# Expert outputs stored by slot, and finished tokens gathered, normed and written inside a hand-ordered expert stretch

## The chip, the cores and the metric

The kernel runs on one NeuronCore of one Trainium2 chip. What is judged is the device time of one execution in microseconds (us), the median of the runs. The engines are PE (TensorE, the matmuls), DVE (VectorE), ACT (ScalarE), POOL (GpSimd) and SP, which here only issues transfers. Each engine takes its own instructions in their written order: an instruction that waits holds up every one behind it on that engine, and nothing else until somebody waits for those.

## The reference

One decoder layer of 1024 tokens of 1024 numbers. Three sub-layers, each `x <- LayerNorm(alpha * x + f(x))`: a mixer (mLSTM and a pooling group), a cross-attention to 256 memory tokens, and a mixture of experts. The change touches the last one and its norm:

```
x = layer_norm(DEEPNORM_ALPHA * x + xa, ln_x_g, ln_x_b)
e = top-2 experts of each token (of 16), gate = their weights
hb = silu(xb @ w_gate[e]) * (xb @ w_up[e])      # 1024 -> 256, per block of 128 tokens of an expert
y  = hb @ w_down[e]                             # 256 -> 1024
ff = sum over the token's two experts of gate * y
x  = layer_norm(DEEPNORM_ALPHA * x + ff, ln_moe_g, ln_moe_b)
```

The norm takes mean and variance over the 1024 numbers of a token, then scales by `g` and adds `b`.

## The kernel before, in words

The stages follow one another: input projection, mixer, memory keys and values, attention scores, attention output with routing, experts, third norm. `yd` is an array in memory that the second norm fills with `alpha * x`.

Experts. Each expert takes its tokens in blocks of 128 slots. There are 24 fixed blocks: the eight busiest experts have two, the other eight one; experts are ordered by how many tokens they have, and a loop behind them (`For_i`, L1511) does what is left if an expert has more; here it makes no turn. Blocks 0 and 1 are done in the stage before; the loop over blocks 2 to 23 is the stretch that this text speaks of. One block is, in the order of its data:

- POOL gathers 128 rows of `xd` by the slot list (`xbs`, L994), PE transposes them (`tp_xb`), ACT rounds them into a high part (L1103) and DVE takes the rest as a low part (`xbT`, L1105);
- PE does 24 matmuls into `gup` (three for each product, high and low parts, L78 to L80), ACT the Silu (`hb`, L1118; called the gate below), DVE the product (L1119, "mult"), PE two transposes (`hp`, L1124, "flip"), ACT and DVE the two parts of the result (`hbT`, L74 and L75), and PE 12 matmuls into `yp`;
- ACT scales `yp` by the slots' weights (`y`, L1145), and POOL adds the rows to `yd` by token, in memory (L1146). Each of these additions waits until the one before has landed, as both write `yd`.

Beside that the weights come in: SP fetches 1 MB at a time into a ring of five buffers (`raw`, L834), and each buffer is split in two pieces into high parts (ACT, L74) and low parts (DVE, L75); a piece is 128x1024, an expert has six, and the loop's experts 84. In this loop the framework's scheduler sets the order of the instructions on each engine.

After the last block some twenty small steps on PE and DVE make the list of the blocks beyond the fixed ones (L1452 to L1485), each engine reads their number, and then the third norm runs: eight loads of `yd` into buffers (`yl`, L1573), statistics on DVE (L1541 to L1543) or ACT (L1545), the power -1/2 on POOL (L1554), the two passes over the row on DVE (L1556, L1558), ACT and POOL (L1564, L1566), and eight stores (L1568), in an order that a string lists by hand.

Of the kernel before, what the change touches and what calls it, by code (L numbers as in the profile page):

```python
# [43 lines left out]
def trunk_kernel(ctx: ExitStack, tc: tile.TileContext, a, out):
# [1401 lines left out]
    def extra_blocks():  # L1446
        def c16(name, n=NE, dtype=F32):
            return const.tile([NE, n], dtype, name=name)

# [29 lines left out]
        for k in range(8):  # L1479
            pe.matmul(lps[:1, :NE], pcol[:, :1], ohx[:, k, :], start=k == 0, stop=k == 7)  # L1480
# [9 lines left out]
    for n in range(2, len(blocks)):  # L1490
# [4 lines left out]
        if n + 1 < len(blocks):  # L1495
            parts = block_parts(gathered[n + 1], f"{n + 1}")
# [130 lines left out]
```

## Time and profile before

| | us |
|---|---|
| median of 3 runs | 996.57 |
| the runs | 992.66, 996.57, 996.59 |
| span of the profiled execution | 991.4 |
| of it the expert loop, up to the last matmul of block 23's first product and block 22's second | up to 939.7 |
| of it from the last small matmul on | 944.5 to 991.4 |
| PE, DVE, ACT, POOL busy in the span | 910.8, 584.9, 410.9, 304.2 |

The profile is of one execution. The page gives its span, from the first instruction to the last, and not the device time of that same execution; the median of the runs lies 5.2 us above the span, the lowest run 1.3. Times inside the span are counted from its start.

### The profile page before, as it was taken

How to read it: one execution, taken by the hardware profiler on the slowest of the kernel's cores; microseconds unless marked ns; L12 is line 12 of the kernel's file. 1: busy time of each engine (PE TensorE's matmuls, PEld its weight loads, DVE VectorE, ACT ScalarE, POOL GpSimd, SP SyncE). 2: the span in 40 equal slices, each digit the busy share in tenths (PEclk: the TensorE clock that was granted, in tenths of full speed). 3: DMA queues.
4: the chain of work that ended last, by engine and by line, in shares of the span. 5: the costliest groups of instructions: out<-in, count | busy, mean ns of one | idle time of the engine just before them, and what ended most of it. 6: DMA issues, size and time to landing. Idle time of an engine off the chain costs nothing. (4 is left out here: it accounts for less than half of the span.)

```text
span 991.4 us, 13027 instructions
## 1 busy us (share of the span) xinstructions
PE 910.8 (92%) x4841; PEld 774.9 (78%) x4841; DVE 584.9 (59%) x1154; ACT 410.9 (41%) x640; POOL 304.2 (31%) x221
## 2 busy tenths in 40 slices
PE   8999999999899999999999999987589999999910
PEld 8999778788677889998888888876468888888710
DVE  5300374546876785272224558979957677676528
ACT  5311432245422144352224432234237667767524
POOL 0211243226453314201111042325732323333226
PEclk9999999999999999999999999999799999999965
DMA  8200011113421357420001012173549898898364
GB/s 304 83 22 22 22 65 43 64 32 128 170 75 54 107 194 273 150 86 0 1 1 43 1 43 86 64 310 108 190 128 347 298 317 290 281 296 270 51 196 167
DMA packets 35439, 133.41 MB, mean 135 GB/s; under 512 B 6640, under 2 KB 8240, under 8 KB 29232
## 3 DMA queue, kind: packets, MB, share of 16 engines
q1 hardware_dynamic: 28464, 115.79, 32.3%
q0 software_dynamic: 6912, 16.79, 7.2%
q8 instruction: 38, 0.62, 0.2%
q14 instruction: 25, 0.20, 0.1%
HBM read 115.75 MB, written 25.20 MB: 142 GB/s over the span
## 5 line engine op out<-in xcount | busy, mean ns | idle before, releaser
L75 DVE TENSOR_TENSOR ew<-raw,ew 128x1024 fp32r<-128x1024 f32 x84 | 101.5, 1223 | 21.7 <-ACT ew L74 20.8
L74 ACT ACTIVATE ew<-raw 128x1024 fp32r<-128x1024 f32 x96 | 100.3, 1057 | 19.4 <-PE xa L80 9.7
L78 PE MATMUL gup<-ew,xbT 128*128 128x512 f32 x192 | 79.2, 412 | 0.0
L1146 POOL DMA_INDIRECT yd<-y,idx x22 | 41.5, 1884 | 122.2 <-ACT ew L74 46.2
L79 PE MATMUL gup<-ew,xbT 128*128 128x512 f32 x192 | 76.7, 399 | 0.0
L80 PE MATMUL gup<-ew,xbT 128*128 128x512 f32 x192 | 76.7, 399 | 0.0
L78 PE MATMUL zB<-xs,wb 128*128 128x512 f32 x192 | 76.5, 399 | 0.0
L80 PE MATMUL zB<-xs,wb 128*128 128x512 f32 x192 | 76.1, 396 | 0.0
L79 PE MATMUL zB<-xs,wb 128*128 128x512 f32 x192 | 75.0, 391 | 0.0
L78 PE MATMUL xa<-vws,T_p 128*128 128x512 f32 x128 | 53.9, 421 | 0.0
L78 PE MATMUL mixp<-wm,mx 128*128 128x512 f32 x128 | 53.2, 415 | 0.0
L79 PE MATMUL mixp<-wm,mx 128*128 128x512 f32 x128 | 50.9, 398 | 0.7 <-DVE wm L75 0.7
L79 PE MATMUL xa<-vws,T_p 128*128 128x512 f32 x128 | 51.4, 401 | 0.0
L80 PE MATMUL xa<-vws,T_p 128*128 128x512 f32 x128 | 51.3, 401 | 0.0
L80 PE MATMUL mixp<-wm,mx 128*128 128x512 f32 x128 | 50.9, 398 | 0.0
L78 PE MATMUL sc<-As,T_x 128*128 128x512 f32 x128 | 50.9, 398 | 0.0
L80 PE MATMUL sc<-As,T_x 128*128 128x512 f32 x128 | 50.4, 394 | 0.0
L79 PE MATMUL sc<-As,T_x 128*128 128x512 f32 x128 | 50.2, 392 | 0.0
L791 POOL TENSOR_TENSOR pss<-pss,nm 128x1024 f32<-128x1024 f32 x8 | 15.1, 1894 | 113.2 <-DVE nm L789 113.2
L80 PEld LDWEIGHTS gup<-ew,xbT 128*128 128x128 f32 x192 | 36.8, 192 | 8.5
L78 PEld LDWEIGHTS gup<-ew,xbT 128*128 128x128 f32 x192 | 37.0, 193 | 7.9 <-issue 0.6
L79 PEld LDWEIGHTS zB<-xs,wb 128*128 128x128 f32 x192 | 36.1, 188 | 8.9 <-issue 0.5
(447 smaller groups left out, 2505.2 us busy)
## 6 DMA issues: line engine op xcount, KB each, us to landing
raw<-in_wgu SPq DMA_DIRECT2D x32, 1024.0 KB, 8.2
raw<-in_wdn SPq DMA_DIRECT2D x16, 1024.0 KB, 7.4
raw_wk<-in_wkv SPq DMA_DIRECT2D x16, 512.0 KB, 4.5
wbr<-in_wB SPq DMA_DIRECT2D x12, 512.0 KB, 3.2
xt<-in_x SPq DMA_DIRECT2D x8, 512.0 KB, 3.2
raw_wq<-in_wxqT SPq DMA_DIRECT2D x8, 512.0 KB, 4.2
xd<-x2s SPq DMA_DIRECT2D x8, 512.0 KB, 3.3
yd<-xal SPq DMA_DIRECT2D x8, 512.0 KB, 2.8
```

Of the source, the lines that this page charges most:

```text
L74: act.activation(hi, src, AF.Copy)
L75: sub.tensor_tensor(lo, src, hi.bitcast(F32), op=ALU.subtract)
L78: pe.matmul(ps, lhi, rhi, start=first, stop=False)
L79: pe.matmul(ps, lhi, rlo, start=False, stop=False)
L80: pe.matmul(ps, llo, rhi, start=False, stop=last)
L791: pool.tensor_tensor(pr4, pr4, nm[:, 1, :, None].to_broadcast([P, H, M]), op=ALU.mult)
L1146: pool.indirect_dma_start(out=yd[:, :], out_offset=bass.IndirectOffsetOnAxis(ap=ix, axis=0), in_=y[:, :D], in_offset=None, bounds_check=T ...
```

## The change

Three things change, all of them from block 2 on; the stages ahead of it keep their work.

- Each block's `y` goes out with a plain store by SP, row by slot, to a new array `yb` of 24 * 128 rows (L1155). Nothing is added to `yd` in the fixed blocks any more.
- From block 4 on a list of some 95 small steps (`late_steps`) is dealt out over the agenda, 0.9 units apart. They work out for each token the two slots where its results lie and the rank of its later expert, sort the tokens by that rank, and write lists (`done`) of nine tiles of tokens: token numbers, first slots, second slots. Two of these steps put groups of small matmuls on PE (`invert`, 8; `listed`, 32), one makes a 128x1024 mask on DVE. The steps on the blocks beyond the fixed ones move here from the end.
- As soon as a tile's tokens have both results, POOL gathers their rows of `yd` and adds those of `yb` (L1458), DVE and POOL norm them (`stats` L593 to L595, the power L599, `vec1` L602, `vec2` L605), and POOL scatters them to the output (L1471). Tiles 8, 7, 6, 5 ("slow") add both `yb` rows in memory transfers and are normed in blocks 18, 19, 21 and 22; tiles 4, 3, 2, 1 ("fast") use freed weight buffers, fetch the second row apart and add it on DVE (`sum`, L1770), in blocks 22 and 23 and after. Tile 0, the tokens of the last expert, takes the last block's result from PSUM (`meet`, L1810).

The stretch is now ordered by an agenda: every step has a time in units (a block is 10 units long, block n starts at `10 * (n - 2)`), and on each engine the instructions stand in the order of these times.

The core of the diff:

```diff
@@ the store of a block @@
-        pool.indirect_dma_start(out=yd[:, :], out_offset=bass.IndirectOffsetOnAxis(ap=ix, axis=0), in_=y[:, :D], in_offset=None,
-                                bounds_check=T - 1, oob_is_err=False, compute_op=ALU.add)
+    def b_store(yp, gc, n):
+        sp.dma_start(yb[n * P:(n + 1) * P, :], b_scaled(yp, gc, f"{n}"))
@@ the gathers of a tile, and its store @@
+    def z_rows(y, src, ix, rows, add=False):
+        pool.indirect_dma_start(out=y, out_offset=None, in_=src[:rows, :], in_offset=bass.IndirectOffsetOnAxis(ap=ix, axis=0),
+                                bounds_check=rows - 1, oob_is_err=False, **(dict(compute_op=ALU.add) if add else {}))
+    def z_add(i, k, n):
+        z_rows(S["z", i], yb, done[:, 1 + k, i:i + 1], n * P, True)
+    def z_store(i):
+        pool.indirect_dma_start(out=out[:, :], out_offset=bass.IndirectOffsetOnAxis(ap=done[:, 0, i:i + 1], axis=0), in_=S["z", i],
+                                in_offset=None, bounds_check=T - 1, oob_is_err=False)
@@ two of the late steps @@
+        def invert():
+            for t in range(NT):
+                pe.matmul(li[:, :3 * NL], slot[:, t * P:(t + 1) * P], val[:, t, :, :].rearrange("p v k -> p (v k)"), start=t == 0, stop=t == NT - 1)
+        yield lambda: vec.tensor_tensor(slot[:, :1024].rearrange("p (t s) -> p t s", s=P), iota[:, None, :].to_broadcast([P, NT, P]),
+                                        rm[:, :, None].to_broadcast([P, NT, P]), op=ALU.is_equal)
@@ a block of the agenda @@
+    SPAN = 10.0
+    for n in range(2, NB):
+        B = start(n)
+        T0 = B - 4.2 if n > 2 else B - 4.0
+        at(T0, e_turn, n)
+        at(T0 + 1.0, e_hi, n)
+        at(T0 + 2.2, e_lo, n)
+        for j, o in enumerate((0.0, 0.7, 1.6, 2.3, 6.7, 7.4, 8.1, 8.8)):
+            at(B + o, e_hidden, n, j)
+        N = B + SPAN
+        at(N + 0.05, e_gate, n)
+        at(N + 0.5, e_mult, n)
+        at(N + 1.5, e_flip, n)
+        at(N + 1.7, e_fold, n)
+        if n < NB - 1:
+            at(N + 3.0, e_out, n, 0)
+            at(N + 4.4, e_out, n, 1)
+            at(N + 5.85, e_store, n)
+    places = [(start(n) + o) for n in range(3, NB) for o in (0.6, 2.0, 3.05, 4.1, 8.05)]
+    for n, step in enumerate(late_steps()):
+        at(start(4) + 5.0 + 0.9 * n, step)
@@ the tiles @@
+        at(B - 3.0 + shift if fast else B, z_x)
+        if fast:
+            at(B + 1.0 + shift, z_add, i, 0, n + 1)
+            at(B + 1.1 + shift, lambda: z_rows(S["zb", i], yb, done[:, 2, i:i + 1], (n + 1) * P))
+            at_z = B + 7.0 + shift
+            at(at_z, z_sum)
+        else:
+            at(B + 6.0, z_add, i, 0, n + 1)
+            at(B + SPAN + 6.0, z_add, i, 1, n + 1)
+            at_z = B + 2 * SPAN + 5.0
+    def z_vec(i, when):
+        at(when, lambda: S.update({("ln", i): ln_stats(S["z", i], f"n3_{i}")}))
+        at(when + 1.6, lambda: ln_pow(S["ln", i][1]))
+        at(when + 1.7, lambda: ln_vec1(S["z", i], S["ln", i][0], gb3))
+        at(when + 3.0, lambda: ln_vec2(S["z", i], S["ln", i][1], gb3))
+        at(when + 4.3, z_store, i)
+    for i, m in ((8, 8), (7, 9), (6, 10), (5, 11)):
+        z_vec(i, z_tile(i, last_of[m]))
+    for i, m, r in ((4, 12, 4), (3, 12, 3), (2, 13, 2), (1, 14, 1)):
+        z_vec(i, z_tile(i, last_of[m], True, fetch_order[r], 4.5 if i == 3 else 0.0))
@@ the last block @@
+        vec.scalar_tensor_tensor(y[:, o:o + 512], S["yp", NB - 1][:, o:o + 512], gc, y[:, o:o + 512], op0=ALU.mult, op1=ALU.add)
+        vec.bn_stats(S["st", 0][:, o // 512, :], y[:, o:o + 512])
```

Where the instructions stand, at three places.

DVE in block 22, before: from the mult of block 21 to that of block 22. `ew15` are the last expert's weights, `xbT` the low part of block 23's tokens, `hbT21` the low part of block 21's hidden row.

```order
L1119 TENSOR_TENSOR hb21_7825<-hb21_7825,gup21_7800 128x256
L75 TENSOR_TENSOR ew15_1_7915<-raw0_5517,ew15_1_7915 128x2x512
L75 TENSOR_TENSOR ew15_2_7918<-raw1_5519,ew15_2_7918 128x2x512
L75 TENSOR_TENSOR ew15_3_7945<-raw1_5519,ew15_3_7945 128x2x512
L1105 TENSOR_TENSOR xbT0_5705<-tp_xb23_7873,xbT0_5705 128x1024
L75 TENSOR_TENSOR hbT21_7859<-hp21_7856,hbT21_7859 128x256
L75 TENSOR_TENSOR ew15_4_7948<-raw2_5521,ew15_4_7948 128x1024
L75 TENSOR_TENSOR ew15_5_7951<-raw2_5521,ew15_5_7951 128x1024
L1119 TENSOR_TENSOR hb22_7909<-hb22_7909,gup22_7884 128x256
```

DVE at the same place now, its second half: ahead of these twelve rows stand block 21's mult, its `hbT`, four pieces and tile 5's `BN_STATS` and `BN_AGGR`. `z5` and `raw3` are tiles 5 and 4.

```order
L595 TENSOR_SCALAR sc_n3_5_8097<-mv_n3_5_8096 128x1
L602 SCALAR_TENSOR_TENSOR z5_7861<-z5_7861,mv_n3_5_8096,g3_7111 128x1024
L1770 TENSOR_TENSOR raw3_5514<-raw3_5514 128x1024
L593 BN_STATS st_n3_4_8135<-raw3_5514 128x6 x2
L594 BN_AGGR mv_n3_4_8132<-st_n3_4_8135 128x2
L595 TENSOR_SCALAR sc_n3_4_8133<-mv_n3_4_8132 128x1
L1661 TENSOR_TENSOR xbT0_5693<-tp_xb23_8110,xbT0_5693 128x1024
L605 SCALAR_TENSOR_TENSOR z5_7861<-z5_7861,sc_n3_5_8097,b3_7112 128x1024
L76 TENSOR_TENSOR ew15_3_8145<-raw1_5510,ew15_3_8145 128x2x512
L602 SCALAR_TENSOR_TENSOR raw3_5514<-raw3_5514,mv_n3_4_8132,g3_7111 128x1024
L605 SCALAR_TENSOR_TENSOR raw3_5514<-raw3_5514,sc_n3_4_8133,b3_7112 128x1024
L1674 TENSOR_TENSOR hb22_8164<-hb22_8164,gup22_8039 128x256
```

Before, seven rows lie between the two mults; now eighteen, the added ones being the norm of tile 5 and the sum and norm of tile 4. Block 23's `xbT` stands behind tile 4's statistics, and block 22's mult behind the last pass of both tiles.

POOL in blocks 17 to 21, before: gathers for the blocks to come (`xbs`) and additions to `yd`, one by turns, then the additions alone.

```order
L994 DMA xbs_5348<-xd_264,idx_6118 128x1024
L1146 DMA yd_265<-y17_7611,idx_6118 1024x1024
L994 DMA xbs_5348<-xd_264,idx_6118 128x1024
L1146 DMA yd_265<-y18_7698,idx_6118 1024x1024
L1146 DMA yd_265<-y19_7775,idx_6118 1024x1024
L1146 DMA yd_265<-y20_7851,idx_6118 1024x1024
L1146 DMA yd_265<-y21_7934,idx_6118 1024x1024
```

POOL in blocks 20 to 22 now. `z5`, `z6`, `raw3`, `raw4` are tiles 5, 6, 4 and 3; L599 is the power -1/2 of tile 6.

```order
L1458 DMA z5_7861<-yd_269,done_6263 128x1024
L1006 DMA xbs_5340<-xd_267,idx_6098 128x1024
L1458 DMA z6_7758<-yb_268,done_6263 128x1024
L1458 DMA z5_7861<-yb_268,done_6263 128x1024
L1006 DMA xbs_5340<-xd_267,idx_6098 128x1024
L1458 DMA z5_7861<-yb_268,done_6263 128x1024
L599 TENSOR_TENSOR sc_n3_6_7991<-sc_n3_6_7991,mhalf_233 128x1
L1458 DMA raw3_5514<-yd_269,done_6263 128x1024
L1471 DMA out_0<-z6_7758,done_6263 1024x1024
L1458 DMA raw3_5514<-yb_268,done_6263 128x1024 x2
L1458 DMA raw4_5516<-yd_269,done_6263 128x1024
L1458 DMA raw4_5516<-yb_268,done_6263 128x1024 x2
```

The power of tile 6 stands behind the second addition into `z5`, which writes the same buffer as the first addition two rows above; tile 6's store stands behind the gather for tile 4.

DVE from the last block's mult on, before: the small steps on further blocks follow, and the norm only behind the reading of the list.

```order
L1119 TENSOR_TENSOR hb23_7979<-hb23_7979,gup23_7954 128x256
L1455 COPY pcol_8027<-pps_8024 16x2
L1460 TENSOR_SCALAR need_8029<-thr_8030,pcol_8027 16x8
L1463 TENSOR_REDUCE nsum_8037<-need_8029 16x1
L1465 SCALAR_TENSOR_TENSOR nscan_8039<-need_8029,z8_8040 16x8
L1464 CAST nrow_8038<-nsum_8037 16x1
L75 TENSOR_TENSOR hbT23_8003<-hp23_8000,hbT23_8003 128x256
L1469 SCALAR_TENSOR_TENSOR nscan_8039<-nscan_8039,xps_8045,need_8029 16x8
L1485 CAST lists_8074<-xps_8045 1x1
```

DVE from the last block's mult on, now. `raw2` and `raw1` are tiles 0 and 1, `yplast` the last block's second product.

```order
L1674 TENSOR_TENSOR hb23_8259<-hb23_8259,gup23_8159 128x256
L76 TENSOR_TENSOR hbT23_8277<-hp23_8274,hbT23_8277 128x256
L1810 SCALAR_TENSOR_TENSOR raw2_5512<-yplast_8280,gsl_6103,raw2_5512 128x512
L1811 BN_STATS st_last_8295<-raw2_5512 128x6
L1810 SCALAR_TENSOR_TENSOR raw2_5512<-yplast_8280,gsl_6103,raw2_5512 128x512
L1811 BN_STATS st_last_8295<-raw2_5512 128x6
L1815 BN_AGGR mv_last_8293<-st_last_8295 128x2
L1816 TENSOR_SCALAR sc_last_8294<-mv_last_8293 128x1
L602 SCALAR_TENSOR_TENSOR raw2_5512<-raw2_5512,mv_last_8293,g3_7111 128x1024
L605 SCALAR_TENSOR_TENSOR raw2_5512<-raw2_5512,sc_last_8294,b3_7112 128x1024
L1770 TENSOR_TENSOR raw1_5510<-raw1_5510 128x1024
L593 BN_STATS st_n3_1_8314<-raw1_5510 128x6 x2
```

The small steps are gone from here. Of the norm seven tiles stand ahead of these rows, tile 0 in them, and tile 1 behind it.

## Rows read from the trace of the kernel before

**Rows 1.** The page, busy us of each engine, share of the span, instructions.

```profile
PE 910.8 (92%) x4841; PEld 774.9 (78%) x4841; DVE 584.9 (59%) x1154; ACT 410.9 (41%) x640; POOL 304.2 (31%) x221
```

**Rows 2.** Busy time by stretch: PE, PEld, DVE, ACT, POOL, clock, DMA share, GB/s.

```profile
745.00:910.00 165.00, 165.00 (x804) 135.75 (x803) 116.40 (x124) 117.83 (x140) 51.91 (x33) 1.00 0.90 299
910.00:939.70 29.70, 29.70 (x141) 24.34 (x140) 16.65 (x19) 16.37 (x21) 7.24 (x4) 1.00 0.48 113
884.10:939.70 55.60, 55.60 (x265) 45.49 (x264) 34.11 (x38) 34.52 (x42) 14.89 (x10) 1.00 0.66 188
944.50:991.40 46.90, 0.79 (x32) 0.68 (x27) 26.01 (x41) 17.64 (x27) 22.33 (x13) 0.53 0.52 190
```

**Rows 3.** The gates by their line, 800 to 945: count, durations, first and last start.

```profile
L1118 ACT ACTIVATE hb<-gup x15: 384/385/386, 806.0 to 937.1; 128x256 f32<-128x256 f32 x15
...
  PE gup L80: 21.8, 15
```

**Rows 4.** DVE by line in the expert stretch: count, busy us, mean ns, idle before.

```profile
L75 DVE TENSOR_TENSOR ew<-raw,ew 128x1024 fp32r<-128x1024 f32 x80 | 96.6, 1223 | 21.0 <-ACT ew L74 20.4
L1105 DVE TENSOR_TENSOR xbT<-tp_xb,xbT 128x1024 fp32r<-128x1024 f32 x20 | 24.4, 1220 | 12.3 <-ACT xbT L1103 12.3
L75 DVE TENSOR_TENSOR hbT<-hp,hbT 128x256 fp32r<-128x256 f32 x21 | 8.8, 419 | 9.2 <-ACT hbT L74 9.2
L1119 DVE TENSOR_TENSOR hb<-hb,gup 128x256 f32<-128x256 f32 x21 | 8.7, 416 | 17.4 <-ACT hb L1118 17.4
```

**Rows 5.** DVE in order of time around block 21: start, us, instruction.

```profile
910.95 0.42 DVE L1119 TENSOR_TENSOR hb<-hb,gup 128x256 f32<-128x256 f32 x1
911.28 1.22 DVE L75 TENSOR_TENSOR ew<-raw,ew 128x1024 fp32r<-128x1024 f32 x1
912.41 1.22 DVE L1105 TENSOR_TENSOR xbT<-tp_xb,xbT 128x1024 fp32r<-128x1024 f32 x1
```

**Rows 6.** DVE in order of time in the third norm.

```profile
959.76 1.28 DVE L1541 BATCH_NORM_STATS2 st_n<-yl 128x6 f32<-128x512 f32 x2
961.08 0.21 DVE L1542 BATCH_NORM_AGGREGATE zs<-st_n 128x2 f32<-128x12 f32 x1
961.32 0.15 DVE L1543 TENSOR_SCALAR zs<-zs 128x1 f32<-128x1 f32 x1
...
961.45 1.28 DVE L1556 SCALAR_TENSOR_TENSOR yl<-yl,zs,g 128x1024 f32<-128x1024 f32 x1
...
963.79 1.28 DVE L1558 SCALAR_TENSOR_TENSOR yl<-yl,zs,b 128x1024 f32<-128x1024 f32 x1
...
969.10 3.36 DVE L1558 SCALAR_TENSOR_TENSOR yl<-yl,zs,b 128x1024 f32<-128x1024 f32 x1 [0.37 <-POOL zs L1554]
...
983.75 1.27 DVE L1556 SCALAR_TENSOR_TENSOR yl<-yl,zs,g 128x1024 f32<-128x1024 f32 x1
984.94 2.47 DVE L1558 SCALAR_TENSOR_TENSOR yl<-yl,zs,b 128x1024 f32<-128x1024 f32 x2
```

**Rows 7.** DVE by line in the attention output, two half-row forms.

```profile
L1258 DVE BATCH_NORM_STATS2 st_n<-x2s 128x6 f32<-128x512 f32 x2 | 1.4, 696 | 0.1
L1257 DVE SCALAR_TENSOR_TENSOR x2s<-x1s,xa 128x512 f32<-128x512 f32 x2 | 1.3, 669 | 0.0
```

**Rows 8.** PE by line at the end of the stretch.

```profile
L80 PE MATMUL yp<-ew,hbT 128*128 128x512 f32 x5 | 2.0, 395 | 0.0
...
L1480 PE MATMUL lps<-ohx,pcol 16*1 16x16 f32 x16 | 0.5, 171 | 0.0
...
L1124 PE MATMUL hp<-ident,hb 128*128 128x128 f32 x2 | 0.4, 272 | 0.0
L1452 PE MATMUL pps<-ip,perm 16*16 16x1 f32 x2 | 0.2, 166 | 0.0
```

**Rows 9.** POOL in order of time at the end.

```profile
941.32 1.55 POOL L1146 DMA_INDIRECT yd<-y,idx  x1 [5.76 <-ACT hbT L74]
947.82 1.55 POOL L1146 DMA_INDIRECT yd<-y,idx  x1 [4.95 <-issue]
961.56 2.12 POOL L1554 TENSOR_TENSOR zs<-zs,mhalf 128x1 f32<-128x1 f32 x2 [12.19 <-DVE zs L1552]
...
967.54 1.53 POOL L1554 TENSOR_TENSOR zs<-zs,mhalf 128x1 f32<-128x1 f32 x1
969.04 2.33 POOL L1566 TENSOR_TENSOR yl<-yl,b 128x1024 f32<-128x1024 f32 x1
```

**Rows 10.** Transfers issued from 728 to 740: issuer, count, median us to landing.

```profile
xbs<-xd,idx POOLq DMA_INDIRECT x4, 5.0
```

**Rows 11.** The same from 740 to 895, with GB/s in 40 slices and the sum.

```profile
GB/s 372 303 386 418 411 339 206 346 296 273 318 317 424 79 239 240 411 389 265 409 218 188 366 239 381 390 242 378 59 256 366 310 333 331 309 208 297 304 320 372
DMA packets 9527, 47.70 MB, mean 308 GB/s; under 512 B 2348, under 2 KB 2348, under 8 KB 5076
...
raw<-in_wgu SPq DMA_DIRECT2D x22, 1024.0 KB, 8.1
...
xbs<-xd,idx POOLq DMA_INDIRECT x16, 9.8
yd<-y,idx POOLq DMA_INDIRECT x15, 9.9
```

**Rows 12.** The same from 915 to 950.

```profile
yd<-y,idx POOLq DMA_INDIRECT x5, 6.1
```

**Rows 13.** The chain that ended last, around the last additions.

```profile
941.32 1.55 DMA yd<-y,idx
942.87 4.74 issue
...
947.82 6.13 DMA yd<-y,idx
...
954.74 3.56 DMA yl<-yd
```

**Rows 14.** SP's last stores, in order of time.

```profile
986.24 1.53 SPq L1568 DMA_DIRECT2D out<-yl  x2
```

More of the change, by code (lines that the diff above doesn't have):

```diff
@@ L40 @@
 NEARLY = 3
+NOSLOT = 1 << 13
 @with_exitstack
@@ L104, in zB @@
         return ps
+    order = list(range(NEARLY))
+    singles = list(range(NDOUBLE, NE))
+    for i in range(NEARLY, NDOUBLE):
+        order += [singles.pop(0), i]
+    order += singles
+    blocks = [(0, 0), (1, 0), (0, 1), (1, 1)] + [(i, k) for i in order[2:] for k in range(2 if i < NDOUBLE else 1)]
+    LASTSLOT = (len(blocks) - 1) * P
     ones = const.tile([P, P], BF16, name="ones")
@@ L171, in trunk_kernel @@
     vec.reciprocal(rc16, rc16)
+    efall, kkall, pmall = [const.tile([P, NT, 2], F32, name=f"{n}all") for n in ("ef", "kk", "pm")]
     xd = dram.tile([T, D], F32, name="xd")
+    yb = dram.tile([len(blocks) * P, D], F32, name="yb")
     yd = dram.tile([T, D], F32, name="yd")
@@ L1488, in trunk_kernel @@
-    parts = block_parts(gathered[2], "2", 512)
-    pend = None
-    for n in range(2, len(blocks)):
-        i, k = blocks[n]
-        last = not any(b[0] == i for b in blocks[n + 1:])
-        wts = experts[f"{i}"]
-        cur = parts
-        if n + 1 < len(blocks):
-            parts = block_parts(gathered[n + 1], f"{n + 1}")
-        if n + 2 < len(blocks):
-            gathered.append(block_gather(col(*blocks[n + 2])[0]))
-        hb = block_hidden(wts, cur, f"{n}")
-        ahead = n if n < 4 else order.index(i) + 1
-        split_some(3, ahead)
-        if pend:
-            block_down(*pend)
-        hT = block_turn(hb, f"{n}")
-        split_some(6 if last else 0, ahead)
-        pend = (wts, hT, *col(i, k), f"{n}")
@@ new lines, in trunk_kernel, with start, e_turn, e_hi @@
+    NB = len(blocks)
+    SPAN = 10.0
+    def start(n):
+        return SPAN * (n - 2)
+    first_of, last_of = {}, {}
+    for n, (i, _) in enumerate(blocks):
+        m = order.index(i)
+        first_of.setdefault(m, n)
+        last_of[m] = n
+    def e_turn(n):
+        S["xb", n] = b_turn(gathered[n], f"{n}")
+    def e_hi(n):
+        S["xbT", n] = s = b_slot()
+        act.activation(s[:, :1024], S["xb", n][:, :], AF.Copy)
+    def e_lo(n):
+        s = S["xbT", n]
+        vec.tensor_tensor(s[:, 1024:2048], S["xb", n][:, :], s[:, :1024].bitcast(F32), op=ALU.subtract)
@@ new lines, in trunk_kernel, with e_piece, e_pieces @@
+    places = [(start(n) + o) for n in range(3, NB) for o in (0.6, 2.0, 3.05, 4.1, 8.05)]
+    pieces = []
+    def e_piece(k, eng):
+        _, piece, last = pieces[k]
+        piece(eng)
+        if last:
+            fetch_some(1)
+    def e_pieces():
+        pieces.extend(splits)
+        del splits[:]
+    at(start(3) - 0.01, e_pieces)
+    k = 0
+    for m in range(2, NE):
+        for q in range(6):
+            free = start(last_of[m - 2] + 1) + (0.5 if q < 4 else 6.0)
+            p = next(p for p in places if p >= free)
+            places.remove(p)
+            at(p, e_piece, k, vec)
+            k += 1
+            need = start(first_of[m]) - 1.0 if q < 4 else start(first_of[m] + 1) + 2.0
+            assert p < need, (m, q, p, need)
@@ L1570, in trunk_kernel @@
[L1570 to L1577 removed]
+        hT = block_turn(hb, "x")
```

340 lines of the change are left out of this document (239 added, 101 removed).

## The prediction

> **What bounds the kernel now.** I read the page first, then stretches, lines and the order of time.
>
> PE is busy 92% of the span [rows 1]. In the expert stretch it never pauses (165.00 of 165.00 us, then 29.70 of 29.70) at the full level of the clock [rows 2], and gates follow each other by (937.1 - 806.0) / 14 = 9.37 us [rows 3]. I use 9.42, the spacing of its middle blocks, as the period. So in this stretch PE sets the time. DVE is busy 116.40 of 165 us, ACT 117.83, and DMA moves 299 GB/s at a share of 0.90 [rows 2]: these have room, DMA little.
>
> Behind it the picture turns. From 944.5 to 991.4 PE does 0.79 us of work [rows 2]; the chain is an addition to `yd`, 4.74 us of waiting for it, another addition that lands after 6.13, a load of 3.56 [rows 13], and the norm up to the last stores, issued from 986.24 [rows 14]. From 939.7, where block 23's first product and block 22's second are done, to the end are 51.7 us. The change goes for these, and pays in the stretch.
>
> The sum is made against the span of 991.4; the median of the runs lies 5.2 above it, and I add 5.2 at the end.
>
> **Prices on DVE.** A piece or an `xbT` part is busy 1.22 [rows 4], but instructions overlap: from 911.28 to 912.41 one takes 1.13, and a mult before it 0.33 [rows 5]. I use 1.15 for a piece, 0.33 for `hbT` and 0.42 for a mult that has waited. A tile's statistics take 959.76 to 961.45, 1.69; a pass follows the next by 984.94 - 983.75 = 1.19, so 1.20 [rows 6], and the added sum, which has no row, is a pass of the same size: 1.2 as well (from 1.15 like a piece to 3.36, the pass beside POOL's large operation [rows 6]; POOL has no such operation here, so the low end). A slow tile costs 1.69 + 2 x 1.20 = 4.09, a fast one 5.29.
>
> **Removed: the tail.** After the change, when PE ends block 23's first product, the mult of block 23 is still to come: DVE has pieces and tiles 3 and 2 ahead of it in its queue. Counted from the start of block 23, DVE's queue is mult .42, two pieces 2.30, `hbT` .33, two sums 2.4, two statistics 3.38, four passes 4.8, with a start at about 0.5 and the mult itself: done at 14.8. PE's product ends at 8.5 (a period less the transposes for a next block, an estimate) + 2.45 (a wait, below) = 11.0, so 3.8 of wait. Then flip 0.4 [rows 8], fold 1.0, the first half of the product 1.6, two halves of 0.67 + 0.70 [rows 7] with the second half of the product hidden under the first, moments 0.36, two passes 2.4, tile 1's 5.29, its store 5.5 to landing (nearest rows 5.0 and 6.1 [rows 10, 12]) and 1 to close: 23.5 in all. Power of tile 0 (0.54 to 1.06 us on POOL, 2.12 for two [rows 9]) lies beside the first pass. 51.7 - 23.5 = **-28.2**.
>
> **Removed: 22 additions to `yd`.** They wait long, but for POOL's own predecessors, and PE never waited for them: 0. The plain stores need ACT's `y` as before, and stand in SP's queue between weight fetches; the ring is about a block and a half ahead, so 0 (up to 3 where a late `y` holds a fetch up).
>
> **Added: the late steps, blocks 4 to 13.** On PE `invert` is 8 matmuls at about 0.19 (the two of L1124 are 0.4 [rows 8]), 1.5; `listed` 32 small ones, 16 of which are 0.5 [rows 8], 1.1; five more 0.3. That is path, as PE has no gap. On DVE some 75 steps of mostly 0.15 to 0.4 fit its 30% of room, but four make PE wait: the mask (1024 wide, 1.2) ahead of `invert`, 1.6 in block 9, and mults that come late behind them, 0.37, 0.57 and 0.35. Together **+5.8** (2.9 if all waits hide, 9 if each of the small steps costs twice).
>
> **Added: the tiles in blocks 18 to 23.** The start of block 18 lies at 939.7 - 5 x 9.42 - 8.5 = 884.1; from there to 939.7 DVE is busy 34.11 of 55.60 us before [rows 2]. The order now holds there 24 pieces (27.6), five `xbT` (5.8), mults and `hbT` (4.8), four slow tiles (16.4) and three fast ones (15.9): 70.5, and DVE can't run ahead, since each block's mult needs PE's product and the next flip needs the mult. By blocks: 18, 19 and 21 have five pieces, `xbT`, mult, `hbT` and a slow tile, 5.75 + 1.15 + .75 + 4.09 = 11.74, with small waits 12.0 against 9.42: +2.6 each, 7.8 (PE waits where `xbT` is late by about 1, and the mult by 1.6). Block 20 has two pieces and no tile: 0. Block 22 has five pieces, `xbT`, tile 5 and all of tile 4: 17.3 against 9.42, +7.85. In block 23 tile 3's sum and statistics stand ahead of block 22's `hbT`, +2.45. Together **+18.1**, 15 to 21 by DVE's pitches.
>
> Without any wait for transfers the span is 991.4 - 28.2 + 5.8 + 18.1 = 987.1.
>
> **Added: waits in POOL's queue.** This has no row of its own. POOL now issues the gathers for the blocks, three per tile, the powers and the stores, all in one queue, and an addition into a tile's buffer waits until the one before it has landed. What stands behind is a power, for which DVE's second pass waits, and behind that DVE's pieces, `xbT` and mults, and so PE. With L the time to landing: tile 7's power is free up to L = 6.7 and late by L - 6.7 beyond; tile 6's is free up to 8.1 and stands behind two landings, 2 x (L - 8.1); in block 22 tile 5's power and tile 4's sum wait 2.3 at L = 5 and 6.8 at 9.5; tile 0's addition is 1.2 late for `meet` at 5, 2.3 at 6.1, 5.7 at 9.5. The trace has L at 5.0 when little else moved [rows 10], 9.8 in the stretch [rows 11], 6.1 when the weights were all in [rows 12]. With 9.5 for tiles 7 and 6, 5 for block 22 and 6.1 for tile 0: 2.8 + 2.8 + 2.3 + 2.3 = **+10.2**. Ends: 0 and 18.1 (9.5 throughout), and a loss of 3 more if PE's clock falls in its new pauses (0.53 was granted in the idle stretch [rows 2]).
>
> The Trainium skill speaks for the low end. Its page "DMA: Bandwidth & Descriptors", section "Anatomy of one DMA — SWDGE (gpsimd) path", gives 2.0 us plus the bytes over 436 GB/s for a transfer that POOL issues; an estimate by it is 3.2 us for 0.5 MB, all waits above would be 0, and the sum 987.1. The trace disagrees beside weight traffic: 9.8 for the same gather [rows 11], and even the quiet ones are at 5.0 [rows 10].
>
> **Forecast:** 991.4 - 28.2 + 5.8 + 18.1 + 10.2 = 997.3, and with 5.2 about 1002.5 us, 0.6% slower: the tail's gain is paid back on DVE and in POOL's queue.
>
> **Rivals.**
> - *Short landings.* The new stretch spreads the transfers out, since the stretch with tiles has slower blocks, and the weights are in by block 21: L is near 5 all through, as in [rows 10]. Waits 3.5, span 990.6, time 995.8: no change; with none at all 992.3. For it: [rows 12]. Against it: [rows 11], and each tile adds three gathers and a store of 0.5 MB.
> - *PE stays the bound (the other side).* The place is DVE's queue in blocks 18 to 23. If late `xbT` and mults find PE with other work (the second product of the block before), the +18.1 shrinks; at 8 or less, with short landings, the span is 991.4 - 28.2 + 5.8 + 8 + 3.5 = 980.5, time 985.7; with nothing left of it 977.7. It decides below +13 of stretch waits. For it: PE's pieces of a block can be taken from either side of the mult. Against it: 70.5 us of DVE in 55.6 of PE is a sum, not an order.
> - *Transfers become the bound.* Before, 1 MB fetches take 8.1 to land at 308 GB/s [rows 11]; in blocks 16 to 21 a block moves 2 MB of weights, 0.5 of tokens, 0.5 of `y` and about 1.5 of a tile and its store, 4.5 MB, which over 12 us are 375 GB/s, above the 308 of [rows 11]. Weights come late and landings grow: waits 18.1 and 4 more for late pieces, span 1009.2, time 1014.4. Against it: the longer blocks lower the demand themselves.
> - *Nothing overlaps:* the steps run, but the gathers wait for each other so that the tiles pile up behind the last block. Then the norm's DVE work comes back to the tail, above 1018.
>
> **Chances.** Forecast 0.42, short landings 0.25, PE stays the bound 0.18, transfers 0.12, pile 0.03. What a measurement of this kernel can tell from no change is about 0.5%, or 991.6 to 1001.5. The forecast's own range, 996 to 1009, gives 0.32 to slower and 0.10 to no change; short landings 0.15 to no change and 0.10 to faster (where the late steps or DVE's rows cost a little less than priced); PE 0.17 to faster and 0.01 to no change; transfers and pile 0.15 to slower. So faster 0.27, no change 0.26, slower 0.47. The range is 980 to 1015: it leaves out the lower half of the PE case and the pile.
>
> **What would show it.** Stretch: PE's busy time from the start of block 18 to the end of block 23's product spread over some 74 us, PE's waits named as DVE `xbT` and `hb`, periods near 12 in blocks 18, 19, 21, and 17 in block 22; DVE at 95% there. POOL: powers waiting for `z` or issue of `z` waiting for DMA; landings of `z` near 9 in blocks 18 to 21. Tail: from block 23's product to the end 23 to 28 us. Wrong if PE's period stays below 10.5 in block 18, if the late steps cost under 3 us of PE, or if landings are under 6.

## The result, and the profile after

The changed kernel is slower, and by more than forecast: median 1030.26 us (1029.48 to 1033.13, 4 runs) against 996.54 for the kernel before, a ratio of 1.0347 (95% interval 1.0324 to 1.0371). The forecast was 1002.5, the range 980 to 1015. The span of the profiled execution is 1028.3 against 991.4, 36.9 more; forecast were 5.9 more.

First the page's busy times, as in [rows 1], then the stretches, as in [rows 2]: from block 2 to the gate of block 17, from there to the gate of block 23, to the last store, and to the end.

```profile
PE 927.4 (90%) x4853; PEld 781.4 (76%) x4853; DVE 610.6 (59%) x1228; ACT 391.2 (38%) x613; POOL 298.1 (29%) x272
```

```profile
735.00:894.65 159.65, 156.92 (x773) 125.73 (x774) 113.34 (x175) 100.44 (x122) 27.68 (x67) 0.98 0.81 298
894.65:987.12 92.47, 65.06 (x268) 50.06 (x266) 64.82 (x79) 38.58 (x47) 40.88 (x30) 0.83 0.87 267
987.12:1015.40 28.28, 5.72 (x14) 3.95 (x14) 16.99 (x24) 1.88 (x3) 13.87 (x12) 0.65 0.54 156
1015.40:1028.30 12.90, 0.00 (x0) 0.00 (x0) 0.00 (x0) 0.00 (x0) 1.01 (x1) 0.50 0.11 42
```

PE still fills the first stretch. In the second it is busy 65.06 of 92.47 us, which took 55.60 before, and the granted clock falls to 0.83. From block 23's gate to the end are 41.2 us (51.7 before from the same point of the work). So, against the forecast's steps, the stretch grew by 10.5 ahead of block 18 (5.8 were forecast) and by 36.9 from there (26.0, with the waits for transfers), and the tail shrank by 10.5 (25.9): 4.7 + 10.9 + 15.4 = 31.0 us amiss.

Who PE waited for, from 735 to 1005 (waiter, waited for: total us, times, longest):

```profile
PE hp L1130 <- DVE hb L1674: 26.5, 7, 9.8
PE gup L81 <- DVE xbT L1661: 10.8, 3, 9.6
PE late L1577 <- DVE lslot L1572: 1.5, 1, 1.5
```

The names are those forecast. But DVE, forecast to be busy 95% of the time from block 18 on, is busy 64.82 of 92.47 us there: it waits itself. DVE in block 22, in order of time, with the idle time ahead of an instruction and what ended it:

```profile
958.29 1.27 DVE L602 SCALAR_TENSOR_TENSOR z<-z,mv_n,g 128x1024 f32<-128x1024 f32 x1
966.89 1.22 DVE L1770 TENSOR_TENSOR raw<-raw 128x1024 f32<-128x1024 f32 x1 [7.33 <-DMA raw<-yb,done]
968.15 1.29 DVE L593 BATCH_NORM_STATS2 st_n<-raw 128x6 f32<-128x512 f32 x2
...
969.79 1.22 DVE L1661 TENSOR_TENSOR xbT<-tp_xb,xbT 128x1024 fp32r<-128x1024 f32 x1
971.80 1.28 DVE L605 SCALAR_TENSOR_TENSOR z<-z,sc_n,b 128x1024 f32<-128x1024 f32 x1 [0.80 <-POOL sc_n L599]
...
976.73 0.41 DVE L1674 TENSOR_TENSOR hb<-hb,gup 128x256 f32<-128x256 f32 x1
```

DVE stands idle 7.33 us for the rows of tile 4, and block 23's `xbT` stands behind the statistics of that tile; PE's third matmul of that block's product waits for it. PE there, in order of time:

```profile
961.04 0.40 PE L80 MATMUL gup<-ew,xbT 128*128 128x512 f32 x1
971.06 0.80 PE L81 MATMUL gup<-ew,xbT 128*128 128x512 f32 x1 [9.62 <-DVE xbT L1661]
...
972.08 0.63 PE L80 MATMUL gup<-ew,xbT 128*128 128x512 f32 x1
```

POOL between tile 5's last addition and tile 4's rows, in order of time:

```profile
946.19 1.53 POOL L1458 DMA_INDIRECT z<-yb,done  x1 [10.72 <-DMA z<-yb,done]
948.50 2.09 POOL L1458 DMA_INDIRECT raw<-yd,done  x1 [0.17 <-issue]
...
955.76 2.48 POOL L1458 DMA_INDIRECT raw<-yb,done  x1 [3.84 <-DMA raw<-yd,done]
958.54 1.93 POOL L1458 DMA_INDIRECT raw<-yb,done  x1 [0.30 <-ACT y L1151]
```

Tile 4's gather (948.50) stands behind an addition that waited 10.72 us for tile 5's buffer, its own addition (955.76) waits for the gather to land, and only behind that comes the fetch (958.54) for which DVE waits. In PE's rows, after 9.62 us of pause the matmuls are busy 0.63 us and follow each other in 0.43, where [rows 8] has 0.39 and the trace before a spacing of 0.23: the granted clock has gone to the lower level.

POOL by line from 860 on (busy us, mean ns, then its idle time before, and for what):

```profile
L1458 POOL DMA_INDIRECT raw<-yb,done x9 | 14.2, 1572 | 16.4 <-DMA raw<-yd,done 15.2 <-DVE sc_n L595 0.6 <-issue 0.3
L1458 POOL DMA_INDIRECT z<-yb,done x8 | 13.7, 1710 | 38.3 <-DMA z<-yb,done 26.7 <-DMA z<-yd,done 8.4 <-DVE hb L1674 3.2
...
L1458 POOL DMA_INDIRECT raw<-yd,done x5 | 7.2, 1438 | 1.2 <-issue 1.0 <-POOL raw L1802 0.3
```

From 860 to the end POOL waits 50.3 us (15.2 + 26.7 + 8.4) for transfers of its own to land before it may issue the next into the same buffer, and 5.7 for a store behind a store (a row not shown). Landings from block 18 to block 23's gate (issuer, count, KB, us):

```profile
raw<-in_wgu SPq DMA_DIRECT2D x5, 1024.0 KB, 13.7
...
raw<-yb,done POOLq DMA_INDIRECT x6, 5.9
z<-yb,done POOLq DMA_INDIRECT x5, 10.7
out<-z,done POOLq DMA_INDIRECT x4, 10.1
```

These medians are near [rows 11] for the slow tiles and [rows 12] for the fast ones, as assumed. The rule that the Trainium skill's page "DMA: Bandwidth & Descriptors", section "Anatomy of one DMA — SWDGE (gpsimd) path", gives, 3.2 us for 0.5 MB as an estimate, is under every median of these.

Last, POOL's last store, then by line the entry of the loop over further blocks (duration ns least/median/most, first and last start) and POOL's drain at the end:

```profile
1015.42 1.01 POOL L1471 DMA_INDIRECT out<-raw,done  x1 [1.61 <-DVEq L1835]
```

```profile
L1835 POOLq EVENT_SEMAPHORE  x17: 17/43/3125, 1015.9 to 1021.9; - x17
...
L1835 POOLq COMPARE_BRANCH  x3: 33/41/45, 1015.8 to 1022.0; - x3
L1835 POOLq INC_SWDGE_SEM  x1: 1360/1360/1360, 1019.4 to 1019.4; - x1
```

```profile
L1906 POOLq DRAIN  x3: 103/179/4881, 1022.2 to 1027.9; - x3
```

From the last store's issue to the end are 12.9 us; the forecast had 6.5.

### The profile page after: what moved, and what is told of

The parts are those of the page before. It is cut to its first block, busy times and chain, and to the rows that moved or that the text cites. A ratio compares the mean times of both kernels' runs of the same rounds, so it can differ in the third digit from the quotient of the medians.

```text
span 1028.3 us, 13119 instructions
## 1 busy us (share of the span) xinstructions
PE 927.4 (90%) x4853; PEld 781.4 (76%) x4853; DVE 610.6 (59%) x1228; ACT 391.2 (38%) x613; POOL 298.1 (29%) x272
## 5 line engine op out<-in xcount | busy, mean ns | idle before, releaser
L75 ACT ACTIVATE ew<-raw 128x1024 fp32r<-128x1024 f32 x96 | 97.7, 1051 | 10.7 <-PE xa L81 10.6
L81 PE MATMUL gup<-ew,xbT 128*128 128x512 f32 x192 | 80.2, 418 | 10.9 <-DVE xbT L1661 10.8
L79 PE MATMUL gup<-ew,xbT 128*128 128x512 f32 x192 | 84.1, 438 | 1.1 <-ACT xbT L1657 1.1
L80 PE MATMUL gup<-ew,xbT 128*128 128x512 f32 x192 | 79.4, 414 | 0.0
L1006 POOL DMA_INDIRECT xbs<-xd,idx x22 | 23.5, 1067 | 125.3 <-PE tp_xb L402 95.1
L81 PEld LDWEIGHTS gup<-ew,xbT 128*128 128x128 f32 x192 | 38.4, 200 | 21.9 <-DVE xbT L1661 12.9
L1661 DVE TENSOR_TENSOR xbT<-tp_xb,xbT 128x1024 fp32r<-128x1024 f32 x22 | 26.9, 1223 | 44.7 <-ACT xbT L1657 44.7
L803 POOL TENSOR_TENSOR pss<-pss,nm 128x1024 f32<-128x1024 f32 x8 | 15.2, 1894 | 113.2 <-DVE nm L801 113.2
L79 PEld LDWEIGHTS gup<-ew,xbT 128*128 128x128 f32 x192 | 38.6, 201 | 8.7 <-ACT xbT L1657 1.5
```

The costliest lines, as they stand in the source:

```text
L75: act.activation(hi, src, AF.Copy)
L79: pe.matmul(ps, lhi, rhi, start=first, stop=False)
L80: pe.matmul(ps, lhi, rlo, start=False, stop=False)
L81: pe.matmul(ps, llo, rhi, start=False, stop=last)
L803: pool.tensor_tensor(pr4, pr4, nm[:, 1, :, None].to_broadcast([P, H, M]), op=ALU.mult)
L1006: pool.indirect_dma_start(out=xb, out_offset=None, in_=xd[:rows, :], in_offset=bass.IndirectOffsetOnAxis(ap=ig, axis=0), bounds_check=rows ...
```

## The experiments

The theory after this result was that POOL's queue holds DVE, and DVE holds PE (A); the rivals were that DVE's work alone fills the stretch (B), and that the transfers as such are the bound (C). All runs change the changed kernel. Times are medians; the ratio to the kernel before follows with its interval.

**No powers.**

```diff
-        at(when + 1.6, lambda: ln_pow(S["ln", i][1]))
-    at(E + 6.3, lambda: ln_pow(S["ln", 0][1]))
```

> The powers of the nine tiles on POOL are left out (the tiles are scaled by the variance itself), all else as in the changed kernel. Theory A (POOL's queue holds DVE): DVE's second passes waited 12.3 us for powers in blocks 18 to 23, and PE behind them, so 10 to 13 us of PE's pauses go, and 2 to 3 us of matmuls at the low clock with them: about 1016 us. Rival B (DVE's own work fills the stretch, and the waits for powers only replace waits that would come anyway): under 4 us go, 1026 or more.

1028.35 (1.0335, 1.0311 to 1.0358), a time as rival B had it. A in this form fell: with the powers gone the periods of blocks 18 and 19 (from a block's gate to the next) are 2.5 and 1.0 us shorter, and the rest is as before. The waits for powers were replaced by others.

**No norm work.**

```diff
-        at(when, lambda: S.update({("ln", i): ln_stats(S["z", i], f"n3_{i}")}))
-        at(when + 1.6, lambda: ln_pow(S["ln", i][1]))
-        at(when + 1.7, lambda: ln_vec1(S["z", i], S["ln", i][0], gb3))
-        at(when + 3.0, lambda: ln_vec2(S["z", i], S["ln", i][1], gb3))
-            at(at_z, z_sum)
```

> Sum, statistics, power and both passes of tiles 8 to 1 are left out; gathers, additions and stores stay. Theory A and B both expect that PE's pauses in blocks 18 to 23 vanish (27.4 us, and 7.8 of low clock), that block 23's product is followed at once (9 us less), and that tile 1's 5 us behind tile 0 go: about 980 us, and 17 periods as before up to block 23, 9.4 each. Rival C (the transfers themselves are the bound, weights come late): periods stay at 11 and more in blocks 18 to 22, and the time above 1005.

1030.74 (1.0353, 1.0328 to 1.0378): all of DVE's work on eight tiles gone, and nothing gained. Both A and B had expected 980, and neither holds in that form. PE ends block 23's product at 965.4 instead of 987.1, and then waits. The waits from 896 to 1020:

```profile
ACT ylast L1151 <- DVE raw L1805: 41.2, 1, 41.2
DVE raw L1805 <- DMA raw<-yb,done: 38.5, 1, 38.5
POOL z L1458 <- DMA z<-yb,done: 25.1, 3, 9.7
...
POOL raw L1458 <- DMA raw<-yd,done: 19.7, 5, 6.2
POOL z L1458 <- DMA z<-yd,done: 14.2, 2, 10.8
POOL out L1471 <- DMA out<-raw,done: 11.0, 3, 5.5
```

DVE's first step on tile 0 waits 38.5 us for tile 0's rows, which stand at the end of POOL's queue; POOL itself waits 70.0 us for landings in these rows. So POOL's queue sets the end without DVE's work on the tiles. Two periods are long here too, 16.4 us from the gate of block 19 and 14.6 from that of block 20: the blocks' own gathers of tokens stand in POOL's queue behind the tiles' transfers, and PE waits 7.5 us for them. Rival C had such periods, and isn't out by this run.

**No additions.**

```diff
-            at(B + 1.0 + shift, z_add, i, 0, n + 1)
-            at(B + 1.1 + shift, lambda: z_rows(S["zb", i], yb, done[:, 2, i:i + 1], (n + 1) * P))
-            at(B + 6.0, z_add, i, 0, n + 1)
-            at(B + SPAN + 6.0, z_add, i, 1, n + 1)
```

> The transfers that add or fetch the rows of yb for tiles 8 to 1 are left out; the gathers of yd, the sums, the norms and the stores stay. Theory A (POOL's queue): the additions that wait for landings are what holds the powers, so the result is near that of the kernel without powers, with the waits of the sums (9.6 us) gone too: 1008 to 1014 us. Rival B (DVE's own work): 1022 or more. Rival C (transfers are the bound): 16 transfers of 0.5 MB less, periods 9.4 to 12 again, landings under 7, under 1010, and raw buffers land earlier than 9 us.

1006.87 (1.0107, 1.0081 to 1.0134). Without the transfers that wait for others, blocks 18 to 21 have periods of 12.04, 12.05, 9.42 and 13.34, the first three just as forecast from DVE's rows. The time lies just under A's range, and also where rival C had it: the landings of `z` and `raw` gathers fell to medians of 6.2 and 4.4 us, as C expected. So this run doesn't tell the order of POOL's queue from the amount of its transfers; the run with POOL's order below does.

**Pauses filled.** The calls of `e_fill`, ahead of block 23's product and of the flips, are not shown.

```diff
+    FILL = {18: 16, 19: 30, 21: 40, 22: 28, 23: 70}
+    def e_fill(ps, n, count):
+        x, w = S["xbT", n], experts[f"{blocks[n][0]}"][0]
+        for _ in range(count):
+            pe.matmul(ps, x[:, :P], w[:, 0, 0, :256], start=True, stop=True)
```

> PE gets matmuls without use in its pauses (16 ahead of block 18's flip, 30, 40, 28 and 70 ahead of those of blocks 19, 21, 22 and 23, 70 ahead of block 23's product; 256 columns each). Theory A': a pause costs twice, since matmuls behind it run at a pitch of 0.43 instead of 0.23 for some us (7.8 us in blocks 18 to 23, 2 in the last product): the low clock goes, and the time falls to 1020 to 1024. Rival: the clock falls whatever PE does there, or the fillers last longer than the pauses: 1030 or more.

1028.25 (1.0327, 1.0303 to 1.0351), not told apart from the changed kernel, between both expectations. The stretch from block 17's gate to block 23's:

```profile
898.69:990.38 91.69, 83.24 (x454) 71.22 (x453) 66.36 (x81) 38.59 (x48) 37.84 (x30) 0.94 0.88 277
```

The clock is 0.94 instead of 0.83, and the stretch 91.69 instead of 92.47 us long. Matmuls at the low clock cost 1.6 us there and in the last product, against 10.0 (spacing of the matmuls above 0.23, summed). So giving the clock back didn't give the time back. The fillers stand in PE's queue themselves, and the periods of blocks 18 and 21 grew (16.4 and 20.7 instead of 14.6 and 17.6), so what the low clock alone costs was not separated from what they cost.

**The table of two by two.** Neither part, and norm work alone. Both leave out the additions as above, and the gather of `yd` and the store; the first leaves out the norm work too. In the second the powers stay on POOL, and POOL clears the slow tiles' buffers:

```diff
-            z_rows(S["z", i], yd, done[:, 0, i:i + 1], T)
-        at(when + 4.3, z_store, i)
```

> Of tiles 8 to 1 nothing is left, neither transfers nor norm work (their rows of the output stay unwritten); the late steps, the plain stores, tile 0 and the end stay. With the run without norm work (POOL alone, 1030.7) and the next one (DVE alone) it makes a table of two by two. Theory D (POOL's queue and DVE's work are two chains side by side, and each alone makes the kernel long): periods of 9.4 after block 9, gate of block 23 near 950, and about 975 to 980 us. Rival F (the late steps, the clock or the end cost the time, not the tiles): above 990.

> The gathers, additions and stores of tiles 8 to 1 are left out, the sums, statistics, powers and passes stay (on whatever lies in the buffers; the slow tiles' buffers are cleared first). Theory D: DVE's work alone, as the sum of its rows has it, stretches blocks 18, 19, 21 to about 12 and 22 to 17, and the time is 1000 to 1006. Rival E (POOL's queue alone is the cost, DVE's work finds room): periods under 10.5, and 980 to 988.

| of tiles 8 to 1 | no norm work | norm work |
|---|---|---|
| no transfers | 975.22 (0.9799, 0.9774 to 0.9824) | 998.71 (1.0031, 1.0013 to 1.0048) |
| transfers | 1030.74 (1.0353) | 1030.26 (1.0347) |

E and F fall; 975.22 lies in D's range of 975 to 980, 998.71 a little under that of 1000 to 1006. Norm work alone costs 23.5 us, transfers alone 55.5, both together 55.0, as of two chains side by side of which the longer sets the time. That the two agree so closely is partly luck: without norm work POOL waits 75 us for landings from 866 on, with it 56, and other waits take their place. And up to 3.1 us of what transfers cost can come from the clock in block 9 (last section), where both runs without transfers had the short period. With neither, the stretch from block 17's gate and the tail:

```profile
894.44:949.43 54.99, 54.95 (x264) 44.32 (x262) 38.20 (x40) 37.64 (x46) 5.14 (x5) 1.00 0.66 246
949.43:973.10 23.67, 3.49 (x14) 2.31 (x14) 6.48 (x10) 1.88 (x3) 4.19 (x3) 0.68 0.14 34
```

PE doesn't pause (54.95 of 54.99), and the tail is 23.7. In the tail, DVE's first step on tile 0 waits for its rows, after PE's last matmul, and POOL's last store follows; then POOL's drain:

```profile
953.90 0.40 PE L81 MATMUL yplast<-ew,hbT 128*128 128x512 f32 x1
957.57 0.75 DVE L1800 SCALAR_TENSOR_TENSOR raw<-yplast,gsl,raw 128x512 f32<-128x512 f32 x1 [5.93 <-DMA raw<-yb,done]
964.09 1.07 POOL L1471 DMA_INDIRECT out<-raw,done  x1 [1.61 <-DVEq L1825]
```

```profile
L1896 POOLq DRAIN  x3: 46/103/2267, 970.0 to 972.8; - x3
```

With norm work alone PE's waits are:

```profile
PE hp L1130 <- DVE hb L1674: 11.6, 5, 4.5
PE gup L81 <- DVE xbT L1661: 4.7, 3, 3.5
```

16.3 us, of which 4.5 come behind block 23's gate. That gate is at 968.55 instead of 949.43, 19.1 later; forecast were 18.1. From block 18 on the periods are 13.55, 10.73, 9.42, 11.98 and 18.95, and DVE is busy 18.50 us of the last.

**POOL's order.** The first run has all work, the second this order without norm work.

```diff
-        at(B - 3.0 + shift if fast else B, z_x)
+        at(B - 3.0 + shift if fast else B - 6.0, z_x)
-            at(B + 1.0 + shift, z_add, i, 0, n + 1)
-            at(B + 1.1 + shift, lambda: z_rows(S["zb", i], yb, done[:, 2, i:i + 1], (n + 1) * P))
-            at_z = B + 7.0 + shift
+            at(B + 1.0 + shift, lambda: z_rows(S["zb", i], yb, done[:, 2, i:i + 1], (n + 1) * P))
+            at(B + 3.5 + shift, z_add, i, 0, n + 1)
+            at_z = B + 9.5 + shift
-            at(B + SPAN + 6.0, z_add, i, 1, n + 1)
-            at_z = B + 2 * SPAN + 5.0
+            at(B + SPAN + 8.5, z_add, i, 1, n + 1)
+            at_z = B + 2 * SPAN + 9.0
```

> All work stays; only times in the agenda change: slow tiles gather yd 6 units earlier, their second addition comes 2.5 later and their norm 4 later; fast tiles fetch the second row before the addition, which comes 2.5 later, and their sum 2.5 later. So fewer transfers stand behind one whose landing they don't need. Theory D: POOL's waits for landings (some 75 us from 866 to 1017) fall by 15 to 25, and so the time, to 1008 to 1016. Rival (transfers are slow because of their number, whatever the order): 1025 or more.

> The run without norm work (1030.7), with the reordered gathers and additions of the run that only changed the agenda. In the run without norm work POOL waited 75 us for landings from 866 to 1017. Theory D (POOL's chain is long because transfers stand behind landings they don't need): the waits fall to 25 or less, and the time to 985 to 1000. Rival G (43 transfers by one queue and their bytes are the cost, in whatever order): above 1015.

With all work 1023.86 (1.0277, 1.025 to 1.0305), 8 us over D's range; without norm work 1009.01 (1.0132, 1.0114 to 1.0149), 21.7 less than in the old order. The number of transfers and their bytes are the same, so the old order, not the amount, cost POOL's chain this much, and rival G (above 1015) falls; how the rest divides between order and amount stays open. The second expectation was still 9 to 24 us too low: POOL's waits for landings fell from 75 to 46 us, not to 25. With all work only 6.4 us of the 21.7 arrive. POOL's waits from 866 to 1015 there:

```profile
POOL out L1471 <- DVE z L605: 18.0, 4, 6.1
POOL sc_n L599 <- DVE sc_n L595: 12.6, 4, 4.7
POOL z L1458 <- DMA z<-yb,done: 10.1, 3, 4.8
...
POOL z L1458 <- DMA yb<-y: 7.7, 1, 7.7
```

Most of the waits for landings have turned into waits for DVE: stores that stand behind a second pass, powers behind statistics. One addition now waits 7.7 us for a block's plain store to `yb`. And 1023.86 is 14.9 us more than the longer of the two parts in this order (1009.01 and 998.71): the two queues aren't only side by side, they also wait for each other.

**All loosened.** The same, with powers, second passes and stores of tiles 8 to 3 later, and with places of their own for the small numbers of a tile's norm (those lines are not shown):

```diff
-        at(when + 1.6, lambda: ln_pow(S["ln", i][1]))
-        at(when + 3.0, lambda: ln_vec2(S["z", i], S["ln", i][1], gb3))
-        at(when + 4.3, z_store, i)
+        late = i > 2
+        at(when + (3.0 if late else 1.6), lambda: ln_pow(S["ln", i][1]))
+        at(when + (5.5 if late else 3.0), lambda: ln_vec2(S["z", i], S["ln", i][1], gb3))
+        at(when + (8.0 if late else 4.3), z_store, i)
```

> All work stays. The reordered agenda (1023.9), and besides for tiles 8 to 3 the power 1.4, the second pass 2.5 and the store 3.7 units later, with the small numbers of a tile's norm in places of their own. In the reordered run POOL waited 18.0 us for second passes ahead of stores and 12.6 for statistics ahead of powers. Theory D': after the landings it is the waits of POOL and DVE for each other that keep the time; most of these 30 us go, half of them on the path: 1006 to 1016. Rival: the sum of both queues' work is the cost, 1020 or more.

1017.3 (1.0219, 1.0195 to 1.0243), between the expectation and its rival. With the same work as the changed kernel two changes of order, with those places, give 13 us back. 18.6 us remain to the norm work alone; how they divide between POOL's own transfers and the waits of the two queues for each other wasn't split.

**No stores, and slow tiles only.**

The first is the run without norm work with one line less, the second the changed kernel without tiles 4 to 1:

```diff
-        at(when + 4.3, z_store, i)
```

```diff
-        z_vec(i, z_tile(i, last_of[m], True, fetch_order[r], 4.5 if i == 3 else 0.0))
```

> The run without norm work (1030.7) without the stores of tiles 8 to 1 as well. A store takes POOL 1.0 and 0.3 us, and three of them waited 11.0 us for the store before to land. Theory D: 8 x 1.3 + 8.5 of waits on the path, about 19 less, 1008 to 1015. Rival (the chain of gathers and additions alone sets the end): 1025 or more.

> Tiles 4 to 1 are left out in full; tiles 8 to 5 keep all their work. With nothing of the eight tiles it was 975.2, with all 1030.3. Theory D: the slow tiles cost the periods of blocks 18 to 22 (14.6, 15.3, 9.4, 17.6 in the changed kernel, 12 to 13 in block 22 without tile 4), so the gate of block 23 is 15 to 18 late, and POOL has no backlog behind it: 990 to 998. Rival (POOL's backlog comes from the slow tiles): above 1005.

Without stores 1010.79 (1.0145, 1.0124 to 1.0167): 19.9 less than with them, as expected; a store behind a store waits for a landing that no data needs (11.0 us in the run without norm work). Slow tiles alone 1001.94 (1.0057, 1.0036 to 1.0078), over the expected range: block 23's gate is 25.0 late instead of 15 to 18, with periods of 14.5, 16.2, 9.4, 17.5 and 9.8 from block 18 on. The sum of rows gives 12.0 for three of these; the rest go with the same waits for POOL as with all tiles (6.8 us of DVE's for powers), and 3.1 come from the low clock ahead of block 9's gate. Each half of the tiles costs about the same, 26.7 and 28.3 us.

**No loop.** The last lines from the reading of the count on are left out.

> The loop over further blocks at the end, which makes no turn, is left out with the reading of its count. In the changed kernel its entry runs from 1015.4 to 1022.0 behind the last store, and POOL's drain to 1027.1. If the entry holds up the drain, the end comes 6 us earlier, 1023 to 1025 us; if the last store's landing is what is waited for, nothing changes, 1029 or more.

1022.95 (1.0285, 1.025 to 1.0319). From the last store's issue to the end:

```profile
1012.70:1019.50 6.80, 0.00 (x0) 0.00 (x0) 0.00 (x0) 0.00 (x0) 1.01 (x1) 0.50 0.19 77
```

6.8 us instead of 12.9: behind the last store the loop's entry costs 6.1 us here. In the kernel before, POOL's part of it ran from 948.2 to 954.8, ahead of the norm and beside the last addition.

No version measured here that does all the work beats the kernel before; the nearest is the loosened one, 2.2% slower.

## Why the prediction was wrong

The step that failed is the term for waits in POOL's queue, +10.2 with ends at 0 and 18.1. Norm work alone and the changed kernel reach block 17's gate together, at 894.4 and 894.6. From there the transfers add 18.4 us up to block 23's gate (92.47 against 74.11; 7.9 were forecast), and 5.3 in the wait for block 23's mult behind it (9.8 against 4.5): 23.7, above the upper end. Nearly all the rest of the 31.9 us between the spans, 996.4 and 1028.3, lies between the last pass and the end (13.2 against 4.7), where tile 1's store and what closes the kernel now follow.

What was wrong in the term is the path, not the landing of a median transfer (10.7 and 5.9, assumed were 9.5 and 5). It priced a wait at each of four places where a power, a sum or tile 0's rows stand right behind a transfer. Of these tile 7's power was late by 2.95 us (2.8 priced) and tile 6's by 3.97 (2.8). But tile 4's sum waited 7.33 and tile 5's power 0.80 (2.3 priced together), and unpriced places came up: tile 2's sum and power, 2.25 and 3.21, ahead of block 23's mult. Tile 0's rows, priced 2.3 late, were not late at all, as PE's last product came after them. Left out was that the queue is one chain from 866 to 1015: about 40 transfers, of which each one that waits delays all later ones, stores that wait for stores among them. Without norm work, tile 0's rows came 38.5 us after the point where DVE was ready for them.

The rival that the gathers wait for each other came nearest in time; it was given 0.03. Its cause is what was seen, its place is not: only tile 1's norm stands behind tile 0's, and the tail shrank.

The other steps:
- The tail without waits, 23.5 to the end. Its terms add up to 24.1, and those of the mult to 14.55 instead of 14.8, which changes little. With neither part the measured 23.7 holds no wait of 3.8 and no tile 1, so by the forecast's terms it should have been 14.4 (15.0 by the terms as listed). The last store's way to the end took 9.0 instead of 6.5. Tile 0's rows came 3.3 behind the product. The product took 3.1, where 1.6 were counted for its first half; in the changed kernel DVE's step on that half starts only at 1003.09, when PE's last matmul of both halves (1002.66, busy 0.39) is done. Gate and mult took 0.9 that the wait had covered, the two passes 3.0 instead of 2.4. In the changed kernel the mult came 5.9 later than forecast, the product took 5.0, most of it at the low clock, and the end 12.9.
- The additions to `yd` at 0 and the plain stores at 0: no wait in the traces before and after speaks against it. (The stores of blocks 0 and 1, in the stage ahead, became plain ones too.) Weights landed in 13.7 us instead of 8.1, but no engine waited for them. The rival that transfers as such are the bound needed late weights, and doesn't explain 21.7 us that the order alone moved; that longer landings have a part in the time isn't excluded.
- The late steps, +5.8. With neither part block 23's product ends at 949.4 instead of 939.7, +9.7. The period up to block 9's gate has 3.1 of it, the pause for the mask (1.5, forecast 1.6) and `invert`; the periods of blocks 4, 6, 7, 9 and 10 have 3.8, where 2.7 were priced. Some 2.1 were there when block 3's gate came (754.19 against 749.33, less 12 matmuls of 0.23 that now stand ahead of it), where nothing was priced; block 2's gate alone varies from 744.3 to 747.2 among the thirteen profiles of changed kernels.
- DVE's work, +18.1: measured alone 19.1. The sum of rows was right, and so were the periods: 13.55 and 10.73 are 24.3 for two of 12.0, and without the additions they were 12.04 and 12.05. Some 4 us of matmuls at the low clock behind the pauses lie in the 19.1, which the forecast had only as a margin of 3; what part of them is on the path was not separated.
- The direction was right, with a chance of 0.47 for slower. What DVE's work costs was right too, but in the changed kernel that cost is hidden behind POOL's.

## What to carry to other kernels

An engine that issues transfers in order is a chain like any other: add up its issues and the landings that it waits for, from its first to its last instruction, and compare that with the span, before pricing single waits. Where two queues wait for each other, cut one out completely and then the other: a part whose removal gains nothing need not be free, it can be the shorter of two chains. Then try the order before the amount: here the same transfers in another order took 21.7 us less without the norm work, and 6.4 less with it. What stands behind the last store counts in full.

## What the runs showed of the hardware

The same pause of PE, 1.50 us in block 9, had three outcomes: from block 8's gate to block 9's it took 12.5 us in four profiles, 14.1 in five and 15.6 in four. The rows show why, first of the run with neither part, then of the run without norm work; PE in order of time:

```profile
807.54 1.06 PE L1577 MATMUL late<-lval,lslot 128*128 128x30 f32 x8 [1.50 <-DVE lslot L1572]
...
809.71 0.40 PE L81 MATMUL yp<-ew,hbT 128*128 128x512 f32 x1
```

```profile
808.46 1.45 PE L1577 MATMUL late<-lval,lslot 128*128 128x30 f32 x8 [1.50 <-DVE lslot L1572]
...
811.60 0.63 PE L80 MATMUL yp<-ew,hbT 128*128 128x512 f32 x1
```

After the same wait the matmuls ran at the higher level in one, busy 0.40, and at the lower in the other, busy 0.63, for 5.7 us. The four profiles with 12.5 were taken together on one chip, and eight of the others on two other chips, where 14.1 and 15.6 both came up on each; so whether the chip has a part in it isn't shown.

POOL's drain at the end grows with the number of transfers that POOL issued in the whole kernel. In the kernels with the loop its longest part took 4.88 us with 59 transfers (seven profiles), 4.23 with 51, 3.57 with 43 (two) and 2.27 with 27 (two), which is 0.08 us for each. `INC_SWDGE_SEM` at the loop's entry went the same way, 1.36, 1.20, 1.04 and 0.72 us. So some 3 us of what the tiles' 32 transfers cost lie behind the last store, in whatever order they are issued.

The entry of a loop that makes no turn cost 6.1 us behind POOL's last store in the changed kernel; without it the drain took 6.14 us instead of 4.88.
